# A three-block decoder layer on one core: the order in which the on-chip pools are laid in each partition

## The chip, the cores and the metric

The kernel runs on one core of one Trainium2 chip. The metric is the device time of one execution in microseconds (us). Three runs of the kernel before gave 2838.76, 2840.28 and 2841.42 us; the median is 2840.28 us.

## The reference

The reference takes 512 tokens of 1024 features, a memory of 256 rows, and runs three blocks one behind the other, all in float32.

- Block 1: a gated feed-forward layer (1024 to 2816 and back) with a layer norm; a pair of mixers side by side (a chunked gated delta rule of 8 heads with short convolutions, and a gated convolution of width 31), gated and joined; cross attention of 4 heads to the memory; a second gated feed-forward layer. Each part ends in a residual sum and a layer norm.
- Block 2: a retention branch and a sparse attention branch (compressed, selected and window keys) of 8 heads each, joined by one output matrix.
- Block 3: a neighbourhood attention branch and a latent attention branch, gated and joined, with a layer norm, and a third gated feed-forward layer with a layer norm.

Nearly all of the arithmetic is products of 512 tokens with weight matrices that are read once:

```python
def swiglu_ffn(x, w_gate, w_up, w_down):
    return (jax.nn.silu(x @ w_gate) * (x @ w_up)) @ w_down

x = layer_norm(DN_ALPHA * x + 0.5 * swiglu_ffn(x, ...), ln1_g[i], ln1_b[i])
proj = h @ w_in        # 1024 x 8208
```

## The kernel before, in words

**Split operands.** Every float32 operand of a large product is held as two tiles of the type float32r, the leading bits (hi) and the rest (lo). `mm3` (lines 192 to 196) makes one product from three matmuls: line 194 takes the lo part of the first operand with the hi part of the second, line 195 hi with lo, line 196 hi with hi. In `PE.matmul(o, lhsT, rhs)` the operand `lhsT` is stationary (128 columns are loaded into the array ahead of the matmul, the rows marked PEld in the profile) and `rhs` is moving (its 512 or 256 columns stream through). The profile names a matmul `mm<-moving,stationary`, so `mm<-x,wh` has an activation tile `x` moving over the weights `wh`, and `mm<-wh,x` has the weights moving over a stationary `x`.

**Weights.** `wload` (lines 269 to 275) fetches 512 KB of weights from HBM by one DMA of the SP queue into a tile `wr` of 1024 floats in each partition; `split` (lines 265 to 267) copies it to `wh` on ScalarE and subtracts to `wl` on VectorE or GpSimd. There are 2 tiles `wr`, 4 `wh` and 4 `wl`, all in the pool `wpool`, for the whole program.

**Activations.** The input of every block is an `Act` of 8 blocks of 128 features by 512 tokens. Those that outlive a phase are made by `xslot` (line 165) in the pool `xpool`: four tiles `x` of 4 blocks each, two for the hi parts and two for the lo parts. All others (`h`, `m`, `ma`, `y`, `ml`, `ra`, `rb`) lie in the pools of a phase, which `room` opens and closes.

**Two shapes of projection.** `feature_proj`, `swiglu` and `by_halves` (lines 306 to 347 and 460 to 487) put out features on partitions: the weights are stationary and 512 tokens of the activation move (256 in `by_halves`, which does the first half of the tokens of some blocks ahead of the second half). `token_proj` (lines 349 to 380) puts out tokens on partitions: 128 tokens of the activation are stationary and 512 columns of weights move. The order of all instructions on each engine's queue is the order in which the Python code emits them; it is written out by hand, in some phases by `interleave` (line 208), which takes turns between two generators by the TensorE time that each has been charged.

**Phases.** Feed-forward 1 is at 0 to about 350 us of the span; the delta rule with the gated convolution to about 800; the mixers' outputs and the cross attention to about 1300; feed-forward 2 to about 1650; block 2 to about 2060; block 3 to about 2480; feed-forward 3 to the end.

**Where tiles lie.** A pool takes a stretch of every partition's bytes, and the stretches follow each other in the order in which the pools are opened, each start rounded up to a multiple of 32 bytes. Four pools on chip are opened at the start (lines 118 to 124), and stay: `cpool` (constants), `xpool` (the four tiles `x`), `ypool` (small tiles and `t1`), `wpool`. The pools of the phases come behind them. In the built program the first pool starts at byte 16,512, and the stretches are:

| pool | first byte | bytes | tiles in it that large matmuls read |
|---|---|---|---|
| `cpool` | 16,512 | 4,640 | `ident` (transposes) |
| `xpool` | 21,152 | 32,768 | `x` |
| `ypool` | 53,920 | 7,208 | none |
| `wpool` | 61,152 | 40,960 | `wr` first, `wh` from 69,344, `wl` from 85,728 |
| pools of the phases | 102,112 | up to 126,464 | `h`, `m`, `ma`, `y`, `ml`, `ra`, `rb` and more |

The tiles `x`, `wr`, `wh`, `wl`, `h`, `m`, `ma` and `y` have 4,096 or 8,192 bytes in a partition, and the slices that a matmul takes of them start at multiples of 512 bytes from the tile's start. (For the 416-column projection of block 3 the step is 1,664 bytes.) So one number for each pool says where an operand starts within any 128 bytes: 32 for `x`, and 96 for the weights and for all tiles of the phases.

Of the kernel before, what the change touches and what calls it, by code (L numbers as in the profile page):

```python
# [14 lines left out]
PSUM = bass.MemoryType.PSUM  # L15
DRAM = bass.MemoryType.DRAM
# [10 lines left out]
BLOCK_STEP = 16 * 128 + 16  # L27
# [61 lines left out]
class Act:  # L89
    """Features on partitions, 512 tokens along: [128, 512] per block of 128 features, split exactly  # L90
    into the 12 leading bits (hi) and what is left (lo)."""
# [17 lines left out]
def kernel(ctx: ExitStack, tc: tile.TileContext, a: dict, out: bass.AP, upto=99):  # L109
# [7 lines left out]

    cpool = ctx.enter_context(tc.tile_pool(name="cpool", bufs=1))
    xpool = ctx.enter_context(tc.tile_pool(name="xpool", bufs=4))
    ypool = ctx.enter_context(tc.tile_pool(name="ypool", bufs=7))  # L120
    dpool = ctx.enter_context(tc.tile_pool(name="dpool", bufs=1, space=DRAM))

# [1 line left out]
    wpool = ctx.enter_context(tc.tile_pool(name="wpool", bufs=1))  # L124

# [1 line left out]
    now = {"lo": V, ("sb", "wr"): (wpool, 2), ("sb", "wh"): (wpool, 4), ("sb", "wl"): (wpool, 4)}  # L127

    class room:
        """SBUF tiles by tag."""  # L130
# [97 lines left out]
    def columns(rows):  # L228
        """Row vectors (dram [n, width <= 128]) turned into columns of one [128, 128] tile."""
        r = t1()  # L230
        V.memset(r, 0.0)
        at = 0
        for key, src in rows:
            n, w = src.shape
            S.dma_start(r[at:at + n, :w], src)
            cols[key] = at
            at += n
        p = tbank((128, T))
        PE.transpose(p[:, :128], r, ident)
        c = cpool.tile([128, 128], FT, name=nm("cols"))  # L240
        A.copy(c, p[:, :128])
        for key, src in rows:
            cols[key] = c[:, cols[key]:cols[key] + src.shape[0]]
# [36 lines left out]
    def to_act(x, act, tt, kk):  # L280
        """Half kk of token rows [128, 1024] into the columns of token tile tt."""
        p = tbank()
        for j in range(4):
            PE.transpose(p[:, j], x[:, (4 * kk + j) * 128:(4 * kk + j + 1) * 128], ident)
        h, l = (t[:, :, tt * 128:(tt + 1) * 128] for t in act.pair(kk))
        split(p, h, l)

    def inv_sqrt(o, x, scale, eps, n):
        """o = (x * scale + eps) ** -0.5"""
        V.tensor_scalar(o, x, scale, eps, OP.mult, OP.add)  # L290
        G.tensor_tensor(o, o, nhalf[:, :n], OP.pow)  # L291

    def layer_norm_rows(y, st, g, b, done):
        """Rows in place, given the statistics of both halves; done(i) after half i."""
        mv = tiny((128, 2), "mv")
        V.bn_aggr(mv, st)
        r = tiny((128, 1), "lr")
        inv_sqrt(r, mv[:, 1:2], 1.0, LN_EPS, 1)
        for i in range(2):
            yh, gh, bh = (t[:, i * 512:(i + 1) * 512] for t in (y, g, b))  # L300
            V.scalar_tensor_tensor(yh, yh, mv[:, 0:1], gh, OP.subtract, OP.mult)  # L301
            V.scalar_tensor_tensor(yh, yh, r, bh, OP.mult, OP.add)  # L302
            done(i)

# [1 line left out]
    def feature_proj(src, c0, nf, act, nk, consume, tag="pj", group=2):  # L306
        """consume(f, psum[128 features, 512]) for nf blocks of 128 columns from c0."""
        f = 0
        while f < nf:
            n = min(group, nf - f)  # L310
            ps = [bank(tag=tag) for _ in range(n)]
            step = 8 // n if nk > 8 // n else nk
            for k0 in range(0, nk, step):
                kn = min(step, nk - k0)
                h, l = wload(src, k0, kn, c0 + f * 128, n * 128)
                for i in range(n):
                    for k in range(kn):
                        cs = slice(i * 128, (i + 1) * 128)
                        mm3(ps[i], (h[:, k, cs], l[:, k, cs]), (act.hi(k0 + k), act.lo(k0 + k)),
                            k0 + k == 0, k0 + k == nk - 1)  # L320
                yield
            for i in range(n):
                consume(f + i, ps[i])
            f += n
            yield
# [3 lines left out]
    def by_halves(jobs, act):  # L329
        """For each (src, c0, banks): one block of 128 columns per bank, all over the first 256 tokens  # L330
        before the others."""
        ws = []
        for src, c0, banks in jobs:
            n = len(banks)
            ws.append(early.pop(0) if early else
                      [wload(src, k0, 8 // n, c0, n * 128, G) for k0 in range(0, 8, 8 // n)])
        for hf in range(2):
            ts_ = slice(hf * 256, (hf + 1) * 256)
            for (src, c0, banks), w in zip(jobs, ws):
                n = len(banks)  # L340
                for i in range(n):
                    cs = slice(i * 128, (i + 1) * 128)
                    for k in range(8):
                        h, l = w[k // (8 // n)]
                        mm3(banks[i][:, ts_], (h[:, k % (8 // n), cs], l[:, k % (8 // n), cs]),
                            (act.hi(k)[:, ts_], act.lo(k)[:, ts_]), k == 0, k == 7)
                yield

    def token_proj(src, c0, cn, act, nk, consume, tail=0, start=0, fine=False):
        """consume(tt, psum[128 tokens, cn]) for cn <= 512 columns from c0; the last `tail` chunks of  # L350
        rows go token tile by token tile."""
        per = max(1, min(nk, 1024 // cn))
# [41 lines left out]
    def block_out(act, nk, src, ys, alpha, norm, key, dest=None, tail=3, start=0):  # L394
        """x = norm(alpha * y + act @ src): rows to DRAM, columns split into a new Act."""
# [52 lines left out]
    def rms_rows(y):  # L448
        """Rows over their rms."""
# [10 lines left out]
    def swiglu(act, wg, gc, wu, uc, scale, h, f0, f1, first=None):  # L460
        """Blocks f0 .. f1 of silu(x wg) * (x wu) * scale."""
# [48 lines left out]
    # ================= first block =================  # L510
# [43 lines left out]
    # -- gated convolution branch --  # L554
# [64 lines left out]
    # -- gated delta rule --  # L619
# [67 lines left out]
    def gdn_rows(h):  # L687
        """q, k, v of one head: projection, short convolution, norms; k and q by features, k decayed and v
        by tokens."""
# [56 lines left out]
    def chunks(t, i):  # L746
        """In a scratch in which blocks of 16 along the diagonals are BLOCK_STEP apart: the chunks of head i."""
        src = t[0:1, 0:1]
        return bass.AP(tensor=src.tensor, offset=src.offset + i * 32 * BLOCK_STEP,
                       ap=[[128, 128], [8 * BLOCK_STEP, 4], [1, 128]])  # L750
# [27 lines left out]
    def gdn_blocks(h):  # L778
        """The inverse within blocks of 16 for heads h and h + 1, one block per partition."""
# [29 lines left out]
    def gdn_head(h):  # L809
# [6 lines left out]
        # blocks of the inverse joined two by two  # L816
# [113 lines left out]
    def gated(key, w, act, nk, bias, tag="pj"):  # L930
        """gate * (act w + bias), in place of the gate."""
# [22 lines left out]
    # -- cross attention --  # L954
# [53 lines left out]
    def soft(ps, P_, gate=None):  # L1008
        """Rows of scores (already scaled) to weights that sum to one (or to the gate)."""
# [62 lines left out]
    # ================= second block =================  # L1072
# [4 lines left out]
    def head_rms(p, nh):  # L1077
        """[128, heads, 64] of psum over its last axis -> 1 / rms, [128, 8]"""
# [15 lines left out]
    def nsa_keys():  # L1094
        """Keys of both branches and groups twice over the partitions, split."""
# [24 lines left out]
    def nsa_queries():  # L1120
        """Queries / 8: hi over lo for even heads, lo over hi for odd ones."""
# [115 lines left out]
    def nsa_attention():  # L1237
        """Heads 2j and 2j+1 share key group j // 2; the parts of one token tile follow those of the next
        one's scores."""
# [33 lines left out]
        def near(j, tt):  # L1273
            """Both branches, at most 256 keys."""
# [91 lines left out]
        units = []  # L1366
# [7 lines left out]
    def staggered(units):  # L1374
        """One more unit starts with every round, in which all that are under way take a step."""
# [12 lines left out]
    def overlapped(units, depth):  # L1388
        """Steps of `depth` consecutive units in turn."""
# [110 lines left out]
    # ================= third block =================  # L1500
    n3 = {}

    def na_q():
        """Queries / 8: hi over lo for even heads, lo over hi for odd ones; tiles of 16 columns by 8 rows."""
# [14 lines left out]
    def na_k():  # L1519
        """Keys: hi twice, lo once."""  # L1520
# [12 lines left out]
    def na_v():  # L1533
        """Values by keys, 8 rows by 32 columns for every tile of queries."""
# [21 lines left out]
    def rpb_tables():  # L1556
        """Relative biases between zeros, in DRAM, one copy of 8 key rows by 64 for every query of a tile; the
        copies lie so that the queries' windows start one stride apart."""
# [14 lines left out]
    def pair_attention(j, tt, scores, v, act, soft_one):  # L1573
        """Heads 2j and 2j+1 for the queries of token tile tt, over all keys."""
# [121 lines left out]
    def rope32(o, x, tt, nh):  # L1696
        """Rotates [128, nh, 32]: the first 16 by the row, the others by the column."""
# [73 lines left out]
    # ================= the program =================  # L1771
# [186 lines left out]
```

## Time and profile before

| what | value |
|---|---|
| median of three runs | 2840.28 us (2838.76 to 2841.42) |
| the profiled execution's own time | 2838.76 us |
| its span, first to last instruction | 2838.8 us |
| TensorE matmuls busy (13,600) | 2704.8 us, 95% of the span |
| TensorE weight loads busy | 2168.1 us, 76% |
| VectorE, ScalarE, GpSimd busy | 1430.9, 1047.9, 471.9 us |
| DMA engines busy, mean | 36.3% for the queue that brings the weights |
| granted TensorE clock, mean | 0.981 |

The span and the profiled execution's own time are the same to within a tenth of a microsecond, so nothing lies around the span. A busy time of matmuls counts overlapping records once. The duration of a single matmul record reaches into the next matmul, since they are pipelined, so the pace of a stretch is read from the distance between starts, not from a record's duration.

### The profile page before, as it was taken

Reading aid. Unit: us, or ns where it says so; the run is one execution under the profiler, and the core shown is the slowest. Engines: PE = TensorE matmul, PEld = TensorE weight load, DVE = VectorE, ACT = ScalarE, POOL = GpSimd, SP = SyncE. Lnnn points to the kernel's source line nnn. Section 1 sums busy time; section 2 is a strip of 40 time slices with the busy share of each in tenths; the row PEclk is TensorE's granted clock in tenths of the full one; section 3 lists DMA queues with packets and bytes.
Section 4 is the critical chain, followed back from the end, with each engine's and each line's share of the span. In section 5 each row is a group of like instructions: output and inputs, shape, how many; then the busy total and the mean of one; then the engine's idle time right before and its main releaser. Section 6 shows DMA issues by size and latency. Waiting matters only on the chain.

```text
span 2838.8 us, 34691 instructions
## 1 busy us (share of the span) xinstructions
PE 2704.8 (95%) x13600; PEld 2168.1 (76%) x13600; DVE 1430.9 (50%) x2516; ACT 1047.9 (37%) x1814; POOL 471.9 (17%) x325
## 2 busy tenths in 40 slices
PE   9999998889788999999999989999999999999998
PEld 7888876667576788888888867775777767888887
DVE  3232368977783456454232365575455464622324
ACT  4222234444443422433222254463256564322221
POOL 0101034343331011001101030131002001211010
PEclk9999999999899999999999999999999999999999
DMA  6333364457444343434333234312235223433322
GB/s 190 93 98 91 97 122 71 73 79 66 89 67 74 77 146 121 141 112 156 96 98 90 96 104 114 95 56 79 84 100 95 55 55 95 161 106 97 96 90 82
DMA packets 326036, 277.29 MB, mean 98 GB/s; under 512 B 50328, under 2 KB 278001, under 8 KB 325873
## 3 DMA queue, kind: packets, MB, share of 16 engines
q1 hardware_dynamic: 317808, 260.40, 36.3%
q10 hardware_dynamic: 8064, 14.68, 1.4%
q8 instruction: 107, 1.75, 0.3%
q14 instruction: 57, 0.46, 0.1%
HBM read 256.64 MB, written 20.49 MB: 98 GB/s over the span
## 4 chain that ended last, share of the span: by engine, by line
PE 47%; DVE 4%; POOL 1%; ACT 1%; DMA 1%; issue 1%; SPq 0%; DVEq 0%; ACTq 0%; POOLq 0%
PE mm L194 13%; PE mm L196 13%; PE mm L195 13%; PE mm L190 5%; DMA wr<-in_w_in 1%; DVE m L302 1%; PE mm L1590 0%; DVE wl L267 0%; ACT wh L266 0%; DVE m L301 0%; POOL t L950 0%; POOL hr L291 0%; PE mm L1348 0%; DVE st L429 0%; DVE m L413 0%
## 5 line engine op out<-in xcount | busy, mean ns | idle before, releaser
L267 DVE TENSOR_TENSOR wl<-wr,wh 128x1024 fp32r<-128x1024 f32 (+1 forms) x351 | 427.3, 1218 | 809.0 <-ACT wh L266 808.2
L194 PE MATMUL mm<-x,wl 128*128 128x512 f32 (+3 forms) x2072 | 809.1, 391 | 23.3 <-DVE xr L711 14.0
L195 PE MATMUL mm<-x,wh 128*128 128x512 f32 (+3 forms) x2072 | 805.0, 389 | 0.0
L196 PE MATMUL mm<-x,wh 128*128 128x512 f32 (+3 forms) x2072 | 804.7, 388 | 0.0
L266 ACT CAST wh<-wr 128x1024 fp32r<-128x1024 f32 (+2 forms) x425 | 436.2, 1027 | 802.6 <-PE mm L196 529.8
L194 PEld LDWEIGHTS mm<-x,wl 128*128 128x128 f32 (+2 forms) x2072 | 394.6, 190 | 109.9 <-DVE xr L711 14.9
L196 PEld LDWEIGHTS mm<-x,wh 128*128 128x128 f32 (+2 forms) x2072 | 394.5, 190 | 85.4 <-issue 2.7
L195 PEld LDWEIGHTS mm<-x,wh 128*128 128x128 f32 (+2 forms) x2072 | 394.9, 191 | 82.2 <-issue 1.9
L267 POOL TENSOR_TENSOR wl<-wr,wh 128x1024 fp32r<-128x1024 f32 x74 | 181.6, 2457 | 440.9 <-ACT wh L266 436.0
L267 POOL TENSOR_TENSOR h<-t,h 128x512 fp32r<-128x512 f32 x66 | 101.6, 1539 | 854.9 <-ACT h L266 854.9
L580 DVE SCALAR_TENSOR_TENSOR ma<-pad,cols,ma 128x512 f32<-128x512 f32 x240 | 227.7, 950 | 9.5 <-ACT ma L578 6.8
L196 PE MATMUL mm<-wh,h 128*128 128x512 f32 x528 | 205.6, 389 | 0.0
L195 PE MATMUL mm<-wl,h 128*128 128x512 f32 x528 | 205.6, 389 | 0.0
L194 PE MATMUL mm<-wh,h 128*128 128x512 f32 x528 | 205.6, 389 | 0.0
L196 PEld LDWEIGHTS mm<-wh,h 128*128 128x128 f32 x528 | 99.1, 188 | 20.6
L194 PEld LDWEIGHTS mm<-wh,h 128*128 128x128 f32 x528 | 99.1, 188 | 20.6
L195 PEld LDWEIGHTS mm<-wl,h 128*128 128x128 f32 x528 | 99.1, 188 | 20.6
L486 ACT ACTIVATE t<-mm 128x512 f32<-128x512 f32 x66 | 39.4, 597 | 132.3 <-PE mm L196 132.3
L487 DVE SCALAR_TENSOR_TENSOR t<-t,mm 128x512 f32<-128x512 f32 x66 | 45.4, 687 | 83.7 <-POOL h L267 57.0
L194 PE MATMUL mm<-m,wl 128*128 128x512 f32 (+1 forms) x224 | 81.8, 365 | 0.1
L196 PE MATMUL mm<-m,wh 128*128 128x512 f32 (+1 forms) x224 | 81.1, 362 | 0.0
L195 PE MATMUL mm<-m,wh 128*128 128x512 f32 (+1 forms) x224 | 81.0, 361 | 0.0
(441 smaller groups left out, 3658.1 us busy)
## 6 DMA issues: line engine op xcount, KB each, us to landing
wr<-in_w_in SPq DMA_DIRECT2D x122, 512.0 KB
wr<-in_ffn_wg SPq DMA_DIRECT2D x44, 512.0 KB
wr<-in_ffn_wu SPq DMA_DIRECT2D x44, 512.0 KB
wr<-in_ffn_wd SPq DMA_DIRECT2D x44, 512.0 KB
wr<-in_w_ffn_in SPq DMA_DIRECT2D x44, 512.0 KB
xd<-m ACTq DMA_DIRECT2D x48, 256.0 KB
m<-xd SPq DMA_DIRECT2D x24, 512.0 KB
wr<-in_w_ffn_out SPq DMA_DIRECT2D x22, 512.0 KB
```

The lines of the kernel that those rows point to most:

```text
L190: PE.matmul(o, lhsT, rhs, start=start, stop=stop)
L194: PE.matmul(o, lh[1], rh[0], start=start, stop=False)
L195: PE.matmul(o, lh[0], rh[1], start=False, stop=False)
L196: PE.matmul(o, lh[0], rh[0], start=False, stop=stop)
L266: A.copy(hi, src)
L267: (eng or V).tensor_sub(lo, src, hi.bitcast(FT))
L302: V.scalar_tensor_tensor(yh, yh, r, bh, OP.mult, OP.add)
L486: A.activation(sg, ps[0][f], AF.Silu)
L487: V.scalar_tensor_tensor(sg, sg, scale, ps[1][f], OP.mult, OP.mult)
L580: V.scalar_tensor_tensor(o, pad[:, j:j + T], tap31(j, c), o, OP.mult, OP.add)
```

## The change

The pools are opened in another order: `wpool` first, then `cpool`, then `ypool`, then `xpool`. `dpool` is in DRAM and takes no place on chip. The diff also deletes the text of comments and docstrings and keeps their lines, so that line numbers stay as they are; that leaves the program as it is.

```diff
+    wpool = ctx.enter_context(tc.tile_pool(name="wpool", bufs=1))
+
     cpool = ctx.enter_context(tc.tile_pool(name="cpool", bufs=1))
+    ypool = ctx.enter_context(tc.tile_pool(name="ypool", bufs=7))
     xpool = ctx.enter_context(tc.tile_pool(name="xpool", bufs=4))
-    ypool = ctx.enter_context(tc.tile_pool(name="ypool", bufs=7))
     dpool = ctx.enter_context(tc.tile_pool(name="dpool", bufs=1, space=DRAM))
 
-    # ---- weights as they come and split, for all phases ----
-    wpool = ctx.enter_context(tc.tile_pool(name="wpool", bufs=1))
-
-    # ---- scratch on chip, laid out anew for every phase ----
     now = {"lo": V, ("sb", "wr"): (wpool, 2), ("sb", "wh"): (wpool, 4), ("sb", "wl"): (wpool, 4)}
```

By the sizes in the table above the stretches become: `wpool` from 16,512, `cpool` from 57,472, `ypool` from 62,112, `xpool` from 69,344, and the pools of the phases from 102,112, where they are now. Within 128 bytes the weights then start at 0, `x` at 96, and the tiles of the phases at 96 as before.

## Rows read from the trace of the kernel before

**Rows 1.** The profile page's line of busy times by engine.

```profile
PE 2704.8 (95%) x13600; PEld 2168.1 (76%) x13600; DVE 1430.9 (50%) x2516; ACT 1047.9 (37%) x1814; POOL 471.9 (17%) x325
```

**Rows 2.** Busy time by stretch: the three feed-forward phases, the delta rule, and the rest. Columns: stretch, its length, then busy time (and number of instructions) of PE, PEld, DVE, ACT and POOL, granted clock, DMA share, GB/s.

```profile
0.00:350.00 350.00, 343.13 (x1566) 281.09 (x1567) 105.13 (x111) 101.78 (x126) 33.71 (x26) 1.00 0.38 114
350.00:800.00 450.00, 386.20 (x2134) 311.00 (x2133) 359.42 (x628) 185.24 (x313) 167.44 (x89) 0.94 0.53 82
800.00:1100.00 300.00, 281.38 (x1382) 229.25 (x1381) 163.70 (x246) 106.81 (x166) 51.51 (x35) 0.96 0.41 94
1300.00:1650.00 350.00, 350.00 (x1548) 285.40 (x1547) 106.60 (x110) 91.51 (x108) 37.42 (x24) 1.00 0.34 104
2480.00:2838.00 358.00, 350.13 (x1520) 284.10 (x1518) 116.90 (x131) 86.38 (x102) 38.00 (x26) 1.00 0.31 96
```

**Rows 3.** A stretch of feed-forward 1 in which `x` moves over weights, 512 columns each: its first and last two matmuls in the timeline of PE (start, duration, both in us).

```profile
30.26 0.39 PE L194 MATMUL mm<-x,wl 128*128 128x512 f32 x1
30.49 0.39 PE L195 MATMUL mm<-x,wh 128*128 128x512 f32 x1
...
147.39 0.39 PE L195 MATMUL mm<-x,wh 128*128 128x512 f32 x1
147.62 0.39 PE L196 MATMUL mm<-x,wh 128*128 128x512 f32 x1
```

**Rows 4.** The groups of PE instructions in the stretch from 30.26 to 147.8 us, by shape, with their number. The three groups of 512 columns are the matmuls of rows 3.

```profile
L194 PE MATMUL mm<-x,wl 128*128 128x512 f32 x168 | 66.2, 394 | 0.0
L195 PE MATMUL mm<-x,wh 128*128 128x512 f32 x168 | 66.2, 394 | 0.0
L196 PE MATMUL mm<-x,wh 128*128 128x512 f32 x168 | 66.2, 394 | 0.0
```

**Rows 5.** The stretch behind it, in which weights move over a stationary `h`, in the same view of PE in order of time.

```profile
147.86 0.39 PE L194 MATMUL mm<-wh,h 128*128 128x512 f32 x1
...
212.93 0.39 PE L196 MATMUL mm<-wh,h 128*128 128x512 f32 x1
```

**Rows 6.** A stretch in which an activation `m` of a phase's pool moves over weights, 512 columns each, in the same view.

```profile
989.42 0.40 PE L196 MATMUL mm<-m,wh 128*128 128x512 f32 x1
...
1058.14 0.39 PE L196 MATMUL mm<-m,wh 128*128 128x512 f32 x1
```

**Rows 7.** A stretch in which weights move over a stationary `x`, in the same view.

```profile
1779.98 0.40 PE L196 MATMUL mm<-wh,x 128*128 128x512 f32 x1
...
1793.04 0.39 PE L196 MATMUL mm<-wh,x 128*128 128x512 f32 x1
```

**Rows 8.** Two stretches with 256 moving columns over weights, `x` in the first and `m` in the second, in the same view.

```profile
394.44 0.28 PE L195 MATMUL mm<-x,wh 128*128 128x256 f32 x1
...
405.44 0.28 PE L196 MATMUL mm<-x,wh 128*128 128x256 f32 x1
...
1158.82 0.28 PE L194 MATMUL mm<-m,wl 128*128 128x256 f32 x1
...
1181.73 0.28 PE L196 MATMUL mm<-m,wh 128*128 128x256 f32 x1
```

**Rows 9.** Busy time in the stretches of rows 5 to 8, to count their matmuls; columns as in rows 2. A matmul that overlaps an edge is counted, so that the numbers of rows 6, 7 and the two of rows 8 hold one matmul ahead of the first row shown.

```profile
147.90:212.90 65.00, 65.00 (x288) 53.83 (x287) 19.83 (x20) 13.17 (x13) 1.93 (x2) 1.00 0.32 95
989.50:1058.20 68.70, 68.70 (x305) 56.85 (x304) 37.92 (x36) 20.92 (x25) 9.05 (x7) 1.00 0.44 140
1158.90:1181.80 22.90, 22.90 (x193) 22.90 (x192) 11.28 (x11) 10.37 (x12) 0.00 (x0) 1.00 0.51 147
394.50:405.50 11.00, 11.00 (x99) 11.00 (x99) 6.15 (x13) 4.36 (x6) 2.65 (x2) 1.00 0.67 209
1780.00:1793.10 13.10, 13.10 (x59) 10.69 (x57) 0.00 (x0) 2.76 (x4) 0.00 (x0) 1.00 0.14 40
```

**Rows 10.** The groups of line 194 in the whole span, by shape, with their numbers; lines 195 and 196 have as many of each. Columns: number, busy time and mean duration of one, idle time ahead and what ended it.

```profile
L194 PE MATMUL mm<-x,wl 128*128 128x512 f32 x1816 | 731.9, 403 | 22.6 <-DVE xr L711 14.0 <-DVE pad L575 6.6 <-ACT rg L1444 2.0
L194 PE MATMUL mm<-wh,h 128*128 128x512 f32 x528 | 205.6, 389 | 0.0
L194 PE MATMUL mm<-x,wl 128*128 128x256 f32 x240 | 70.9, 295 | 0.7 <-DVE wl L267 0.7
L194 PE MATMUL mm<-wh,x 128*128 128x512 f32 x160 | 65.1, 408 | 0.5 <-DVE x L1092 0.2 <-ACT wh L266 0.2
L194 PE MATMUL mm<-m,wl 128*128 128x512 f32 x160 | 63.7, 398 | 0.1
L194 PE MATMUL mm<-wh,m 128*128 128x512 f32 x104 | 41.1, 395 | 0.2 <-ACT t L1013 0.2
L194 PE MATMUL mm<-wh,y 128*128 128x512 f32 x64 | 25.1, 393 | 1.2 <-DVE m L940 1.2
L194 PE MATMUL mm<-wh,ma 128*128 128x512 f32 x64 | 25.0, 391 | 0.0
L194 PE MATMUL mm<-ml,wl 128*128 128x512 f32 x32 | 12.5, 390 | 0.0
```

**Rows 11.** The instructions that write or read a tile `x`, busy in the stretch of the delta rule; columns: PE, PEld, DVE, ACT, granted clock, DMA share, GB/s.

```profile
350.00:800.00 450.00, 290.78 (x1149) 209.25 (x1149) 5.30 (x8) 4.69 (x8) 0.94 0.53 82
```

## The prediction

> **What bounds the kernel now.** I began with the busy times: TensorE's matmuls are in flight for 95% of the span, and no other engine is over 50%, weight loads aside [rows 1]. Then I cut the span into phases. In feed-forward 2 TensorE is busy for 350 of 350 us, in the other two feed-forwards for all but 7 and 8 us, always at granted clock 1.00, the 2.4 GHz level; in the delta rule it is busy for 386 of 450 us, and VectorE for 359 [rows 2]. So outside the delta rule the time is a count of matmuls times the distance from one start to the next, and the question is what that distance hangs on.
>
> It is not the same everywhere. In 117 us of feed-forward 1 there are 3 x 168 matmuls that move 512 columns of `x` over weights, so 503 distances between 30.26 and 147.62 us [rows 3, 4]: 117.36 / 503 = 233.3 ns each. Right behind it weights move over `h`: (212.93 - 147.86) / 287 = 226.7 ns [rows 5, 9]. Shape, type, clock and the rate of fetched weights are alike. The orientation is not the reason: where `m` moves over the same weights, as `x` does, the distance is (1058.14 - 989.42) / 303 = 226.8 ns [rows 6, 9]. With `x` stationary it is (1793.04 - 1779.98) / 57 = 229.1 ns [rows 7, 9]. With 256 columns it turns round: `x` moves at (405.44 - 394.44) / 97 = 113.4 ns, `m` at (1181.73 - 1158.82) / 191 = 119.9 ns [rows 8, 9]. Apart from the stationary `x`, all these are whole multiples of 6.67 ns: 35, 34, 34, 17 and 18. 16 columns of four bytes, 64 bytes, take 6.67 ns at 2.4 GHz. So I read them as so many 64-byte pieces per matmul: 32 pieces for 512 columns, and two or three more. All operands now start 32 bytes past a multiple of 64, so that 512 columns touch 33 pieces; the last one or two come from how the read of the moving operand falls against the load of the next weights. What sets `x` apart from `m`, `h` and the weights is its place: it starts 32 bytes into a stretch of 128 bytes, all the others 96.
>
> **The change, part by part.** Instructions, their order, the DMAs, queues and waits: nothing is added, removed or moved. The four pools are opened before any tile is asked for, stay to the end, and fill the same bytes together; the pools of the phases begin at 102,112 as now, so the reuse of their tiles and its waits stay. SP's, ACT's and POOL's queues issue what they issue now. This is priced at nothing, and nothing has to cover it.
>
> What moves is where four kinds of tiles start. Constants and small tiles go in no long run of matmuls: nothing. The weights come to start at a multiple of 64 bytes (and of 128), and `x` comes to start at 96 of 128, as `m` and `h` do. That touches these matmuls [rows 10], three of each group counted there:
>
> 1. *`x` moving, 512 columns: 3 x 1816 = 5448.* Now 233.3 ns. No row shows the new pair, a moving operand at 96 over weights at 0. The near end is 226.7, if the place of `x` itself decides, for then it is `m`'s row; the other end is 233.3, if the two operands must lie alike within 128 bytes, for `x` and the weights differ now and differ after. I take 226.7: the moving operand, with 33 pieces, is the one whose pace is counted, and its new start is exactly that of `m` [rows 6]. 5448 x 6.6 = 36.0 us less.
> 2. *Weights moving over `h`, `m`, `y`, `ma`: 3 x (528 + 104 + 64 + 64) = 2280.* Now 226.7. An aligned start needs 32 pieces and not 33; if this counts in full it is 220.0, if the surplus is the load's it stays. No row has an aligned moving operand of this kind. I take the middle, 3.3 ns: 2280 x 3.3 = 7.5 us less (0 to 15).
> 3. *Weights moving over `x`: 3 x 160 = 480.* Now 229.1; `x` becomes like `h`, so 220.0 at best as in 2, and 229.1 at worst. I take 3.3 ns: 1.6 us less (0 to 4.4).
> 4. *`x` moving, 256 columns: 3 x 240 = 720.* By the argument of 1 it becomes `m`'s row: 6.6 ns more, 4.8 us more (0 to 4.8).
> 5. *`m` and `ml` moving over weights: 3 x (160 + 32) = 576.* The moving operand stays; I take nothing, between 6.6 ns less and 6.6 more: 3.8 us either way.
>
> Cover: in the delta rule 1149 instructions of PE have an `x` [rows 11], so 7.6 us of term 1 at most lie there. TensorE is idle for 64 us of that phase [rows 2] and some matmuls with `x` fill the time in which it would wait for VectorE. I count half as lost, 3.8 us. In the feed-forwards nothing hides behind TensorE: VectorE has 105 to 117 us of work in 350, ScalarE 86 to 102, DMA 31 to 38% [rows 2], so a matmul 3% quicker meets no new bound; what is late next is still the matmul.
>
> Sum: -36.0 - 7.5 - 1.6 + 4.8 + 3.8 = -36.5 us. The profiled execution's own time is 2838.8 us, 1.5 us under the median of the runs shown; 2838.8 - 36.5 = 2802.3, and I say **2802 us**.
>
> **The ports by the Trainium skill.** The rows show two paces for one shape and one clock, 233.3 and 226.8 ns, over the same weights [rows 3, 6]. The Trainium skill, "TensorE: Matmul & The Clock Gate", section "Step-by-step: what each phase is for", says that TensorE has two independent read ports into SBUF, so that loading the next weights takes no bandwidth from the running matmul. By that rule where the tiles lie is worth nothing, and the time would be 2838.8 us. The trace does not agree in so far as the place of `x` goes with 6.6 ns.
>
> **The rivals.** *Only the weights gain.* The pair decides, `x` and weights stay opposed within 128 bytes. `x` stays at 233.3 and 113.4; weights moving get their full piece, 2280 x 6.7 = 15.3 and 480 x 6.7 = 3.2; `m` over weights becomes opposed, 576 x 6.5 = 3.7 more. 2838.8 - 14.8 = 2824. For it: the 256-column rows show that no operand is slow by itself. *Both reads get shorter.* The weights' load, too, has a piece less when it starts aligned (8 and not 9). Then `x` falls to 33 pieces, 220.0: 5448 x 13.3 = 72.5, with 15.3 and 4.4 beside it, and about 8 lost in the delta rule: some 84 less, 2755. Against it: every row has at least one surplus piece. *Low bytes are slow.* `x` lies lowest of all large operands now; then the weights inherit that. `x` moving becomes the pace of today's stationary one, 229.1: 5448 x 4.2 = 22.9 less; weights moving become 233.3: 2280 x 6.6 + 480 x 4.2 = 17.0 more; term 5 pays 576 x 2.3 = 1.3. 2834. Against it: with 256 columns `x` is the quick one. *No effect,* as by independent ports, or because the profile's starts differ for another reason: 2839. Against it is the steadiness, 503 distances without one out of line. *Slower.* The opposition spreads and alignment gives no piece back. The place is TensorE's moving read beside its weight load: weights moving over `h` pay what they pay over `x`, 2280 x 2.4 = 5.5; `m` pays what `x` pays, 3.7; `x` keeps 233.3 and may pay more. 2848 or above. It decides if the distance of `x` over weights stays above 231.6 (9.2 us / 5448 = 1.7 ns under today's). For it: no row has a pair at 0 and 96, and 64 bytes apart was the worse one in two of three shapes.
>
> **How the numbers follow.** Forecast, between 2784 and 2822: 0.47. Only the weights: 0.22. Both shorter: 0.08. Low bytes: 0.06, and 0.04 for no effect; slower 0.13. Leaving out "both shorter" and "slower" leaves about 0.79, from the forecast's lower bound, widened by terms 2 and 5 and half of the way to the deep case, to no effect: 2768 to 2842. A measurement of this kernel can tell about 0.2%, 5.7 us, from no change. Faster is the forecast, only the weights and both shorter: 0.77; within 0.2% are low bytes and no effect: 0.10; slower 0.13. The first three have the sign in common; within the likeliest alone the range is 2784 to 2822.
>
> **What would show it.** Right: the same counts of instructions in all groups; in feed-forward 1 the stretch of 504 matmuls with `x` takes 114 us and not 117.4, at 226.7 ns; the stretch of 288 with `h` at 220 to 226.7 ns; 256 columns of `x` at 120. The phases with TensorE at 100% shorten by 2 to 3%, the delta rule by less. Wrong: `x` at 233.3, which is "only the weights" if `h` falls to 220, and "slower" if `h` goes to 229; `x` at 229 and `h` at 233, which is low bytes. Wrong in another way would be a change of engine durations or of waits for DMA, since this prices neither.

## The result, and the profile after

The change makes the kernel slower by about half a per cent: 2855.39 us, the median of four runs (2853.92 to 2856.71), against 2840.85 us for the kernel before (2838.76 to 2843.42). The ratio is 1.0055, 95% interval 1.0043 to 1.0068. The forecast was 2802 us, with a range from 2768 to 2842, so the sign and the range were wrong. The profiled execution took 2854.75 us, its span is 2852.9 us, and the mean granted clock was 0.983 (0.981 before).

The instructions stand in the same order on every engine, and their counts are the same. The page's line of busy times, to hold against [rows 1]:

```profile
PE 2726.2 (96%) x13600; PEld 2174.7 (76%) x13600; DVE 1434.7 (50%) x2516; ACT 1047.6 (37%) x1814; POOL 473.5 (17%) x325
```

TensorE's matmuls are busy for 21.4 us more; its weight loads moved by 6.6 us, and no other engine by more than 4. TensorE's idle time fell from 2838.8 - 2704.8 = 134.0 to 2852.9 - 2726.2 = 126.7 us, so 7.3 us of the extra time lies where it used to wait, and 14.1 us lengthen the span. By stretch, with the columns of [rows 2]:

```profile
0.00:350.00 350.00, 344.23 (x1547) 281.16 (x1548) 103.60 (x108) 100.83 (x125) 33.82 (x26) 1.00 0.35 113
350.00:800.00 450.00, 386.59 (x2101) 310.77 (x2100) 358.34 (x613) 183.15 (x304) 168.74 (x89) 0.93 0.52 82
```

In 350 us of feed-forward 1, TensorE is as busy as before and gets through 1547 matmuls, not 1566. Some 6 of these 19 are due to a start that is 1.5 us later; the others are missing because the matmuls themselves are further apart. The timeline of PE has the first and last matmul of the stretches of [rows 3], [rows 5], [rows 8] and [rows 6], and of [rows 7]:

```profile
31.74 0.40 PE L194 MATMUL mm<-x,wl 128*128 128x512 f32 x1
...
149.11 0.39 PE L196 MATMUL mm<-x,wh 128*128 128x512 f32 x1
149.34 0.39 PE L194 MATMUL mm<-wh,h 128*128 128x512 f32 x1
...
216.57 0.40 PE L196 MATMUL mm<-wh,h 128*128 128x512 f32 x1
...
399.52 0.28 PE L195 MATMUL mm<-x,wh 128*128 128x256 f32 x1
...
411.15 0.28 PE L196 MATMUL mm<-x,wh 128*128 128x256 f32 x1
...
995.22 0.40 PE L196 MATMUL mm<-m,wh 128*128 128x512 f32 x1
...
1065.91 0.39 PE L196 MATMUL mm<-m,wh 128*128 128x512 f32 x1
...
1167.98 0.28 PE L194 MATMUL mm<-m,wl 128*128 128x256 f32 x1
...
1190.90 0.28 PE L196 MATMUL mm<-m,wh 128*128 128x256 f32 x1
...
1793.22 0.40 PE L196 MATMUL mm<-wh,x 128*128 128x512 f32 x1
...
1806.58 0.39 PE L196 MATMUL mm<-wh,x 128*128 128x512 f32 x1
```

Divided by the same numbers of distances as before, these give:

| matmuls | before, ns | after, ns |
|---|---|---|
| `x` over weights, 512 columns | 233.3 | 117.37 / 503 = 233.3 |
| weights over `h`, 512 | 226.7 | 67.23 / 287 = 234.2 |
| `m` over weights, 512 | 226.8 | 70.69 / 303 = 233.3 |
| weights over `x`, 512 | 229.1 | 13.36 / 57 = 234.4 |
| `x` over weights, 256 | 113.4 | 11.63 / 97 = 119.9 |
| `m` over weights, 256 | 119.9 | 22.92 / 191 = 120.0 |

What was to become quick stayed slow, and what was quick became slow.

### The profile page after: what moved, and what is told of

Same layout as the page of the kernel before. It is cut to its first block, busy times and chain, and to the rows that moved or that the text cites. A ratio compares the mean times of both kernels' runs of the same rounds, so it can differ in the third digit from the quotient of the medians.

```text
span 2852.9 us, 34691 instructions
## 1 busy us (share of the span) xinstructions
PE 2726.2 (96%) x13600; PEld 2174.7 (76%) x13600; DVE 1434.7 (50%) x2516; ACT 1047.6 (37%) x1814; POOL 473.5 (17%) x325
## 4 chain that ended last, share of the span: by engine, by line
PE 48%; DVE 4%; POOL 1%; ACT 1%; issue 1%; DMA 0%; DVEq 0%; SPq 0%; POOLq 0%; ACTq 0%
PE mm L194 13%; PE mm L196 13%; PE mm L195 13%; PE mm L190 5%; DVE m L302 1%; PE mm L1590 0%; DVE m L301 0%; POOL t L950 0%; PE mm L1348 0%; DVE st L429 0%; DVE m L413 0%; DMA wr<-in_w_in 0%; POOL hr L291 0%; DVE wl L267 0%; PE mm L284 0%
## 5 line engine op out<-in xcount | busy, mean ns | idle before, releaser
L196 PE MATMUL mm<-wh,h 128*128 128x512 f32 x528 | 209.5, 397 | 0.0
L194 PE MATMUL mm<-wh,h 128*128 128x512 f32 x528 | 209.4, 397 | 0.0
```

Of the source, the lines that this page charges most:

```text
L194: PE.matmul(o, lh[1], rh[0], start=start, stop=False)
L196: PE.matmul(o, lh[0], rh[0], start=False, stop=stop)
```

## The experiments

Each of the ten kernels differs from the kernel before only in the order of the pools on chip and in unused tiles (`gap1`, `gap2`) that shift what follows; e9 also lengthens a tile. The edits are shown against the kernel before. To follow them, two numbers are needed: where an operand starts, and how far the start of the moving operand is from that of the stationary one. The table has both within 256 bytes, worked out as in the table of pools; `ph` stands for all tiles of the phases. Two operands are called alike when their distance is 0.

| kernel | `x` | weights | `ph` | `x` over weights | weights over `ph` | `ph` over weights | ratio to before (95%) |
|---|---|---|---|---|---|---|---|
| before | 160 | 224 | 224 | 192 | 0 | 0 | 1 |
| after | 224 | 128 | 224 | 96 | 160 | 96 | 1.0055 (1.0043 to 1.0068) |
| e1 | 224 | 224 | 224 | 0 | 0 | 0 | 0.9914 (0.9899 to 0.9929) |
| e2 | 0 | 0 | 0 | 0 | 0 | 0 | 0.9920 (0.9905 to 0.9935) |
| e3 | 96 | 224 | 96 | 128 | 128 | 128 | 1.0049 (1.0033 to 1.0066) |
| e4 | 64 | 128 | 128 | 192 | 0 | 0 | 0.9998 (0.9988 to 1.0008) |
| e5 | 224 | 224 | 224 | 0 | 0 | 0 | 0.9907 (0.9888 to 0.9927) |
| e6 | 224 | 224 | 160 | 0 | 64 | 192 | 0.9937 (0.9915 to 0.9958) |
| e7 | 224 | 192 | 96 | 32 | 96 | 160 | 1.0065 (1.0045 to 1.0086) |
| e8 | 224 | 0 | 64 | 224 | 192 | 64 | 1.0047 (1.0032 to 1.0063) |
| e9 | 224 | 224, `wl` 0 to 192 on | 224 | mixed | mixed | mixed | 0.9997 (0.9985 to 1.0010) |
| e10 | 160 | 128 | 224 | 32 | 160 | 96 | 1.0057 (1.0040 to 1.0074) |

**e1: half of the change.** `xpool` and `ypool` change places and the weights stay where they were, so that `x`, weights and phases start alike.

```diff
-    xpool = ctx.enter_context(tc.tile_pool(name="xpool", bufs=4))
     ypool = ctx.enter_context(tc.tile_pool(name="ypool", bufs=7))
+    xpool = ctx.enter_context(tc.tile_pool(name="xpool", bufs=4))
```

> Only the order of two pools is undone against the kernel before: constants, small tiles, x, weights. The weights and all tiles of the phases stay where they were before; x moves up by 7,232 bytes and now starts at 96 within 128 bytes, as all other operands do. Theory A, the pair must start alike within 128 bytes: x moving over weights goes from 233.3 to 226.7 ns, with 256 columns from 113.4 to 120 ns, weights over x from 229.1 to 226.7: -36.0 + 4.8 - 1.2 us, a few of them lost in the delta rule, so about 2812 us. Theory B, operands in the low bytes (under some 60,000) are slow: x still lies at 28,384 to 61,152, so 233.3 and 113.4 ns stay and the time is 2841 us.

Measured: 2814.46 us, where the kernel before took 2839.47. The page's line of busy times:

```profile
PE 2678.9 (95%) x13600; PEld 2173.7 (77%) x13600; DVE 1436.6 (51%) x2516; ACT 1047.9 (37%) x1814; POOL 473.3 (17%) x325
```

and the stretches with `x` moving 512 and 256 columns in the timeline of PE:

```profile
30.59 0.40 PE L193 MATMUL mm<-x,wl 128*128 128x512 f32 x1
...
144.63 0.39 PE L195 MATMUL mm<-x,wh 128*128 128x512 f32 x1
...
388.25 0.28 PE L194 MATMUL mm<-x,wh 128*128 128x256 f32 x1
...
399.88 0.28 PE L195 MATMUL mm<-x,wh 128*128 128x256 f32 x1
```

114.04 / 503 = 226.7 ns: `x` takes the pace that `m` and `h` had. With 256 columns it is 119.9, where it was 113.4 before. So half of what the change does is a gain of 0.9%, and what turns it into a loss is the move of the weights. `x` still lies below the weights, as in the kernel before, which speaks against "low bytes are slow".

**e2: alike, at another start.** As e1, with 32 unused bytes ahead of `xpool`, so that all large operands start at a multiple of 256.

```diff
-    xpool = ctx.enter_context(tc.tile_pool(name="xpool", bufs=4))
     ypool = ctx.enter_context(tc.tile_pool(name="ypool", bufs=7))
+    gap1 = ctx.enter_context(tc.tile_pool(name="gap1", bufs=1)).tile([128, 8], FT, name="gap1")
+    xpool = ctx.enter_context(tc.tile_pool(name="xpool", bufs=4))
```

> As the run with everything at 96, with 32 bytes left free ahead of x, so that x, the weights and all tiles of the phases start at a multiple of 128 bytes. Theory A with nothing else: all pairs alike, so the same distances as there, 226.7 and 120 ns, and about 2812 us. Theory A with the count of 64-byte pieces: an aligned start saves a piece of each moving operand, 220.0 ns with 512 columns and 113.4 with 256, on some 9000 matmuls, 60 us less: about 2755 us. Theory B: x is still low, 2841 us.

Measured: 2816.99 us, which can't be told from e1. The timeline of PE, `x` over weights and weights over `h`:

```profile
30.75 0.40 PE L194 MATMUL mm<-x,wl 128*128 128x512 f32 x1
...
144.79 0.39 PE L196 MATMUL mm<-x,wh 128*128 128x512 f32 x1
145.02 0.39 PE L194 MATMUL mm<-wh,h 128*128 128x512 f32 x1
...
210.07 0.39 PE L196 MATMUL mm<-wh,h 128*128 128x512 f32 x1
```

Both are at 226.7 ns (114.04 / 503 and 65.05 / 287). An aligned operand gives back no 64-byte piece: where operands start is worth nothing by itself, as far as these two kernels go.

**e3: alike within 128 bytes only.** Weights first, `x` and the phases 128 bytes off them within 256.

```diff
+    gap1 = ctx.enter_context(tc.tile_pool(name="gap1", bufs=1)).tile([128, 24], FT, name="gap1")
+    wpool = ctx.enter_context(tc.tile_pool(name="wpool", bufs=1))
     cpool = ctx.enter_context(tc.tile_pool(name="cpool", bufs=1))
-    xpool = ctx.enter_context(tc.tile_pool(name="xpool", bufs=4))
     ypool = ctx.enter_context(tc.tile_pool(name="ypool", bufs=7))
+    gap2 = ctx.enter_context(tc.tile_pool(name="gap2", bufs=1)).tile([128, 8], FT, name="gap2")
+    xpool = ctx.enter_context(tc.tile_pool(name="xpool", bufs=4))
...
-    wpool = ctx.enter_context(tc.tile_pool(name="wpool", bufs=1))
```

> The changed order (weights first) with 96 bytes left free ahead of the weights and 32 ahead of x, so that weights, x and the tiles of the phases all start at 96 within 128 bytes; the weights stay low in the partition. Within 512 bytes the weights start at 224 and the others at 352, so they are not alike there. Theory A: 226.7 ns for x, m and h with the weights, about 2812 us. Theory B, low bytes: weights low, so all pairs stay as in the changed kernel, 233.3 and 234.3 ns, 2855 us. If alike within 512 bytes is what counts: not 226.7.

Measured: 2854.62 us, as slow as the change. The timeline of PE, `x` over weights and weights over `h`:

```profile
31.61 0.39 PE L195 MATMUL mm<-x,wl 128*128 128x512 f32 x1
...
148.49 0.40 PE L197 MATMUL mm<-x,wh 128*128 128x512 f32 x1
148.72 0.40 PE L195 MATMUL mm<-wh,h 128*128 128x512 f32 x1
...
215.69 0.39 PE L197 MATMUL mm<-wh,h 128*128 128x512 f32 x1
```

116.88 / 503 = 232.4 ns, and weights over `h` are at 66.97 / 287 = 233.3. The prediction counted starts within 128 bytes, and by that count these operands are alike. Either the period is longer than that, or weights that lie low are slow. e3 alone leaves this open.

**e4: the relations of before, at other starts.**

```diff
-    xpool = ctx.enter_context(tc.tile_pool(name="xpool", bufs=4))
     ypool = ctx.enter_context(tc.tile_pool(name="ypool", bufs=7))
+    gap1 = ctx.enter_context(tc.tile_pool(name="gap1", bufs=1)).tile([128, 24], FT, name="gap1")
+    xpool = ctx.enter_context(tc.tile_pool(name="xpool", bufs=4))
+    gap2 = ctx.enter_context(tc.tile_pool(name="gap2", bufs=1)).tile([128, 16], FT, name="gap2")
```

> The order constants, small tiles, x, weights, with free bytes so that the weights and the tiles of the phases start at 0 within 128 bytes and x at 64: every operand starts at a multiple of 64 bytes, and x is opposed to the weights by 64. Theory A: weights over h and m over weights alike, 226.7 ns (220.0 if an aligned start saves a piece); x over weights unlike, 233.3 ns (226.7 if it saves one), with 256 columns 113.4. Time 2841 us, or with the piece about 2785. Theory B: as in the kernel before, 2841 us.

Measured: 2840.02 us against 2839.47, no change. The timeline of PE:

```profile
31.72 0.39 PE L195 MATMUL mm<-x,wl 128*128 128x512 f32 x1
...
149.08 0.40 PE L197 MATMUL mm<-x,wh 128*128 128x512 f32 x1
149.31 0.40 PE L195 MATMUL mm<-wh,h 128*128 128x512 f32 x1
...
214.38 0.39 PE L197 MATMUL mm<-wh,h 128*128 128x512 f32 x1
```

233.3 and 226.7 ns, the paces of before, with every large operand 96 bytes further back within 256. The paces went with the distance between the two operands and not with where they start. The changed kernel and e1 say the same of `x` from the other side: in both it starts at 224, and over the weights it takes 233.3 ns in the one and 226.7 in the other. So the place of `x`, the prediction's reason for its largest term, does not set its pace.

**e5: weights first, as in the change, but all alike.**

```diff
+    gap1 = ctx.enter_context(tc.tile_pool(name="gap1", bufs=1)).tile([128, 24], FT, name="gap1")
+    wpool = ctx.enter_context(tc.tile_pool(name="wpool", bufs=1))
     cpool = ctx.enter_context(tc.tile_pool(name="cpool", bufs=1))
-    xpool = ctx.enter_context(tc.tile_pool(name="xpool", bufs=4))
     ypool = ctx.enter_context(tc.tile_pool(name="ypool", bufs=7))
+    gap2 = ctx.enter_context(tc.tile_pool(name="gap2", bufs=1)).tile([128, 104], FT, name="gap2")
+    xpool = ctx.enter_context(tc.tile_pool(name="xpool", bufs=4))
...
-    wpool = ctx.enter_context(tc.tile_pool(name="wpool", bufs=1))
```

> The changed order, weights first and low in the partition, with 96 bytes left free ahead of the weights and 416 ahead of x, so that the weights, x and the tiles of the phases all start at 224 within 512 bytes. Theory C, only the difference between the starts of the moving and the stationary operand counts, taken within 512 bytes: zero everywhere, so 226.7 ns with 512 columns, 120 ns with 256, and about 2814 us as with everything at 96 in the unchanged place. Theory D, weights that lie low in the partition are slow, wherever they start: distances of 232 to 234 ns stay, about 2855 us.

Measured: 2813.41 us against 2838.54. The timeline of PE, `x` over weights:

```profile
32.34 0.40 PE L195 MATMUL mm<-x,wl 128*128 128x512 f32 x1
...
146.38 0.39 PE L197 MATMUL mm<-x,wh 128*128 128x512 f32 x1
```

226.7 ns again. The weights lie as low as in the change, and the order of the pools is the change's own. This settles what e3 left open: it is not the place low in the partition. e1, e2 and e5, the three kernels with all operands alike, can't be told from each other, and all three beat both the kernel before and the change (e6 does too, by less).

**e6, e7, e8: the size of the step.** All three have `cpool`, `ypool`, `xpool`, then an unused tile, `wpool` and another unused tile. The gaps are 256 and 192 bytes in e6 (shown), 480 and 160 in e7, 288 and 64 in e8.

```diff
-    xpool = ctx.enter_context(tc.tile_pool(name="xpool", bufs=4))
     ypool = ctx.enter_context(tc.tile_pool(name="ypool", bufs=7))
+    xpool = ctx.enter_context(tc.tile_pool(name="xpool", bufs=4))
+    gap1 = ctx.enter_context(tc.tile_pool(name="gap1", bufs=1)).tile([128, 64], FT, name="gap1")
+    wpool = ctx.enter_context(tc.tile_pool(name="wpool", bufs=1))
+    gap2 = ctx.enter_context(tc.tile_pool(name="gap2", bufs=1)).tile([128, 48], FT, name="gap2")
...
-    wpool = ctx.enter_context(tc.tile_pool(name="wpool", bufs=1))
```

> Order constants, small tiles, x, 256 free bytes, weights, 192 free bytes, phases. Moving minus stationary within 512 bytes: x over weights 256, m over weights 192, weights over h 320 (minus 192). Theory C with a period of 512: x not alike, about 232 to 234 ns, so 2840 us or more. Theory C with a period of 256: x alike, 226.7 ns, and weights over h as a difference of 64, 229.1 ns, m over weights as minus 64, 233.3 ns: about 2823 us. Theory D: weights high, so 226.7 ns for all that start where they like, 2814 us.

Measured: 2821.16 us. The timeline of PE, `x` over weights, weights over `h`, and `m` over weights:

```profile
31.96 0.40 PE L195 MATMUL mm<-x,wl 128*128 128x512 f32 x1
...
146.00 0.39 PE L197 MATMUL mm<-x,wh 128*128 128x512 f32 x1
146.23 0.39 PE L195 MATMUL mm<-wh,h 128*128 128x512 f32 x1
...
211.92 0.39 PE L197 MATMUL mm<-wh,h 128*128 128x512 f32 x1
...
983.77 0.40 PE L197 MATMUL mm<-m,wh 128*128 128x512 f32 x1
...
1054.47 0.39 PE L197 MATMUL mm<-m,wh 128*128 128x512 f32 x1
```

`x`, now 256 bytes off the weights within 512, is at 226.7 ns, as if alike. Weights over `h`, 64 off within 256 and 320 within 512, are at 65.69 / 287 = 228.9, where weights over `x` were at 229.1 before with 64 within both. So with 512 columns the period is 256. `m`, 192 off, is at 70.70 / 303 = 233.3 ns, which is the pace that `x` had at 192 before. So the same distance makes the same price for another tile.

> Order constants, small tiles, x, 480 free bytes, weights, 160 free bytes, phases. Moving minus stationary within 512 bytes: x over weights 32, m over weights 160, weights over h minus 160. Theory C does not say what half a 64-byte piece does: between 226.7 (a piece is what counts) and 234.3 ns (any difference counts) for x; weights over h as in the changed kernel, 232 to 234 ns. So 2830 to 2868 us. Theory D: 226.7 ns, 2814 us.

Measured: 2856.68 us. The timeline of PE, `x` at 32 and `m` at 160:

```profile
31.27 0.40 PE L195 MATMUL mm<-x,wl 128*128 128x512 f32 x1
...
148.63 0.39 PE L197 MATMUL mm<-x,wh 128*128 128x512 f32 x1
...
991.47 0.39 PE L197 MATMUL mm<-m,wh 128*128 128x512 f32 x1
...
1062.45 0.40 PE L197 MATMUL mm<-m,wh 128*128 128x512 f32 x1
```

233.3 and 234.3 ns. 32 bytes off already cost the whole price.

> Order constants, small tiles, x, 288 free bytes, weights, 64 free bytes, phases. Moving minus stationary within 512 bytes: x over weights 224, m over weights 64, weights over h minus 64. Theory C: weights over h take 233.3 ns, as x over weights did at minus 64 in the kernel before; m over weights 229.1 ns, as weights over x did at 64; x somewhere from 226.7 to 234.3 ns. So 2830 to 2870 us. Theory D: 2814 us.

Measured: 2852.08 us. The timeline of PE, `x` at 224 and `m` at 64:

```profile
30.86 0.39 PE L195 MATMUL mm<-x,wl 128*128 128x512 f32 x1
...
148.22 0.40 PE L197 MATMUL mm<-x,wh 128*128 128x512 f32 x1
...
990.69 0.39 PE L197 MATMUL mm<-m,wh 128*128 128x512 f32 x1
...
1060.04 0.39 PE L197 MATMUL mm<-m,wh 128*128 128x512 f32 x1
```

233.3 and 228.9 ns. One tile does not fit. `ml`, which block 3 moves over weights and which e8 puts at 64 too, takes (2414.1 - 2392.4) / 93 = 233.3 ns, counted from its first matmul on line 195 to its last there:

```profile
L195 PE MATMUL mm<-ml,wl x32: 397/397/398, 2392.4 to 2414.1; 128*128 128x512 f32 x32
```

Put together from e1 to e8, e10 and the two kernels, with the distance taken as the start of the moving operand less that of the stationary one, within 256 bytes:

| distance, bytes | 512 columns, ns | 256 columns, ns |
|---|---|---|
| 0 | 226.7 | 120.0 |
| 32 | 233.3 | 116.7 |
| 64 | 228.9 to 229.1, `ml` 233.3 | 117.8 |
| 96 | 233.3 | 120.0 |
| 128 | 232.4 to 233.3 | 118.6 |
| 160 | 234.2 to 234.4 | 118.7 |
| 192 | 233.3 | 113.4 for `x`, 117.8 for `m` in e6 |
| 224 | 233.3 | 118.3 |

For 512 columns one number says nearly all: alike is best, 64 bytes is near it but for `ml`, everything else costs 6 to 8 ns. For 256 columns it does not: at 192 there are two paces. Within 512 bytes the two differ, `x` being at 448 there and `m` in e6 at 192; no run tells whether that, or something else about the tiles, makes the difference.

**e9: which of the two weights counts.** As e1, with the tiles `wl` 64 bytes longer than needed, so that the four of them start at 0, 64, 128 and 192 bytes from the rest. One matmul in three with `x` moving (line 193 here, 194 before) then has, in three cases of four, unlike weights of its own, and another has them loaded behind it.

```diff
-        raw, hi, lo = work("wr", (128, 1024)), work("wh", (128, 1024), FR), work("wl", (128, 1024), FR)
+        raw, hi, lo = work("wr", (128, 1024)), work("wh", (128, 1024), FR), work("wl", (128, 1040), FR)
```

> The kernel with everything at 96 (constants, small tiles, x, weights), but each tile wl has 64 bytes more, so that the four wl tiles start 0, 64, 128 and 192 bytes on within 256 bytes, while wr, wh, x and the phases are alike. Line 194 then has an unlike stationary operand in three of four cases, lines 195 and 196 none. Theory P, a matmul's distance hangs on its moving operand and its own weights: the distance from line 194 to line 195 goes from 226.7 to 229 to 233 ns, the two others stay. Theory N, it hangs on its moving operand and the weights that are loaded meanwhile, those of the matmul behind it: the distance from line 196 to the next line 194 grows, and that from line 194 to 195 stays. By both the time is about 10 us over that kernel, 2824 us (1816 x 3.7 ns for x over wl, 984 x 3.7 ns for wl over the others).

Measured: 2839.16 us, 15 us above the 2824 that was expected. The page's line of busy times has PE at 2702.6 us, 23.7 more than e1:

```profile
PE 2702.6 (95%) x13600; PEld 2175.6 (77%) x13600; DVE 1437.0 (51%) x2516; ACT 1048.0 (37%) x1814; POOL 474.3 (17%) x325
```

The timeline of PE, `x` over weights:

```profile
31.74 0.40 PE L193 MATMUL mm<-x,wl 128*128 128x512 f32 x1
...
147.48 0.40 PE L195 MATMUL mm<-x,wh 128*128 128x512 f32 x1
```

115.74 / 503 = 230.1 ns. Sorted by the distance of `x` over its `wl` (64 where `wl` lies 192 further on), over the whole span and without the distances above 260 ns, the mean from start to start is:

| `x` over `wl`, bytes | from its own matmul to the next, ns | from the matmul ahead of it to its own, ns |
|---|---|---|
| 0 | 227.5 | 227.9 |
| 64 | 233.4 | 230.7 |
| 128 | 233.8 | 232.4 |
| 192 | 235.2 | 229.3 |

The third distance of each triple, with alike weights on both sides, is 228.3. So unlike weights lengthen two distances, the one in which they are in use and the one in which they come to be used, and neither a theory of a matmul's own weights nor one of the next weights is enough. For the same reason the table above holds only where all the weights lie alike: a distance of 64 for `wl` alone costs 5.9 ns and 2.8 here, where 64 for all weights cost 2.2 to 2.4 a matmul. The expectation priced one distance of the three, and the expected loss was too small for that. (230.1 - 226.7) x 5448 = 18.5 us is the price for `x`; `wl` moving over `h` pays beside it.

**e10: the other half of the change.** Weights first, `xpool` and `ypool` in their old order.

```diff
+    wpool = ctx.enter_context(tc.tile_pool(name="wpool", bufs=1))
     cpool = ctx.enter_context(tc.tile_pool(name="cpool", bufs=1))
...
-    wpool = ctx.enter_context(tc.tile_pool(name="wpool", bufs=1))
```

> Half of the change: the weights go first, x and the small tiles keep their order (weights, constants, x, small tiles), no free bytes. Moving minus stationary within 256 bytes: x over weights 32, m over weights 96, weights over h minus 96, weights over x minus 32. By the distances of the runs so far, theory C with a period of 256: x 233.3 and, with 256 columns, 116.7 ns, m 233.3, weights over h 234.3, weights over x 233.3 ns; that is the changed kernel but for 720 x 3.3 = 2.4 us, about 2853 us. Theory D, low weights are slow, is out by the run with weights first and alike; if x is what costs when it follows the weights, this kernel is quicker than 2841 us.

Measured: 2854.20 us, where the table of distances gave 2853. The timeline of PE:

```profile
31.41 0.39 PE L193 MATMUL mm<-x,wl 128*128 128x512 f32 x1
...
148.76 0.40 PE L195 MATMUL mm<-x,wh 128*128 128x512 f32 x1
149.00 0.39 PE L193 MATMUL mm<-wh,h 128*128 128x512 f32 x1
...
216.23 0.39 PE L195 MATMUL mm<-wh,h 128*128 128x512 f32 x1
```

233.3 and 234.2 ns. The loss of the whole change is all in this half. The swap of `xpool` and `ypool`, worth 0.9% alone (e1), is worth nothing once the weights have been moved to 128, 96 bytes off the tiles of the phases.

## Why the prediction was wrong, point by point

**What bounds the kernel.** Right. The time is a count of matmuls by the distance between their starts, and the starts of the operands set this distance. VectorE and ScalarE are as busy as before (1434.7 and 1047.6 us).

**Term 1, `x` moving, 36.0 us less: the step that failed.** It chose between two ends, the place of `x` itself and the relation of `x` to the weights, and took the first. The second holds. Before, `x` was 192 off the weights, after it is 96 off, and both cost 233.3 ns, so that nothing came of the 36.0 us. The prediction named this end, and dropped it because the moving operand was "the one whose pace is counted"; that reason did not come from a row. The rows that could have spoken were there: weights over `x`, the same two tiles in the other roles, were at 229.1 where weights over `h` were at 226.7. A theory of the moving operand alone has no place for this difference. Nor do the paces come in whole pieces of 6.67 ns, as the prediction read them: 228.9 and 232.4 ns are 34.3 and 34.9 of them.

**Term 2, weights over `h` and its like, 7.5 us less.** Wrong in sign. No aligned piece exists (e2). The weights were alike with these tiles, and the change took that away: 2280 x (234.2 - 226.7) = 17.1 us more, outside the range of 0 to 15 less that was given. This is the larger part of the loss.

**Term 3, weights over `x`.** 480 x (234.4 - 229.1) = 2.5 us more, not 1.6 less, for the same reason.

**Term 4, 256 columns of `x`.** Right in number, 119.9 ns, 4.7 us more; but not by its reason, since in e7 `x` has the same start, 224, and is at 116.7 ns, 32 off the weights.

**Term 5, `m` and `ml`.** Its bad end came: 576 x 6.5 = 3.7 us more.

**Sum and cover.** 0 + 17.1 + 2.5 + 4.7 + 3.7 = 28.0 us at the full paces, and some 1.4 more for weights over `ra` and `rb` (192 matmuls at 7.5 ns), which the five terms leave out; the span grew by 14.1. The starts of the same matmuls before and after show where the rest went. Ahead of the first long stretch there are 1.5 us (30.26 to 31.74): 144 matmuls of term 4 stand there, 0.9 us, and the rest does not go with the pace, for this start lies at 30.59 in e1 and at 32.34 in e5. At 394.44 the lag is 5.1 us, at 989.42 it is 5.8. Between them lie the delta rule and most of the mixers' outputs, but only 98 matmuls of term 4 and 80 of term 5, 1.2 us at the full paces, so there was little to cover. At 1158.82 it is 9.2. At 1779.98, behind feed-forward 2, it is 13.2, and 4.0 of this is what 528 weights over `h` cost at 7.5 ns; the matmuls between these two starts cost 8.2 us at the full paces, by their counts, so half of that was covered. In feed-forward 3 the groups of weights over `h` have these ranges of starts, before:

```profile
L194 PE MATMUL mm<-wh,h x176: 388/389/397, 2598.3 to 2829.3; 128*128 128x512 f32 x176
```

and after:

```profile
L194 PE MATMUL mm<-wh,h x176: 391/397/400, 2608.8 to 2843.8; 128*128 128x512 f32 x176
```

The lag is 10.5 us at the first and 14.5 at the last: again 4.0 in the phase, while blocks 2 and 3 gave back 2.7 and hid some 6.6 us that their matmuls cost at the full paces. TensorE has idle time there, in block 2 of the kernel after 17.3 us (columns of [rows 2]):

```profile
1650.00:2060.00 410.00, 392.73 (x2109) 289.59 (x2108) 236.63 (x579) 182.24 (x439) 77.89 (x69) 1.00 0.29 88
```

So about half of the loss was covered, the share that the prediction took for its gain in the delta rule, but here it was found for the most part in the cross attention and in blocks 2 and 3. What TensorE waited for there is not shown.

**The rivals.** "Slower" came true, by its own sign: `x` over weights stayed above 231.6 ns, and `m` paid what it priced. Its 2848 was too low because it priced weights over `h` at 229.1, the one cheap distance that the rows before showed; the change made it 234.2. It was given 0.13. "Only the weights gain" had the relation right, and the period and the aligned piece wrong: e3 and e2 speak against these. "Low bytes" falls with e5, "both reads get shorter" with e2. "No effect" falls with all of them: e1 and e3 run the same instructions on the same data and differ by 40.2 us. The rule of the Trainium skill beside which it stood, "TensorE: Matmul & The Clock Gate", section "Step-by-step: what each phase is for", with its two independent read ports, does not account for this either: in e9 the distance behind a matmul whose own weights are alike grew from 227.9 to 232.4 ns when the next weights were 128 off. Whether it is the weight load that disturbs the running matmul, or something else that hangs on the pair, no run here shows.

**What stays open.** Why the distance within 256 bytes matters, and why 64 is nearly free for most tiles and not for `ml`, is not shown; nor what gives 256 columns two paces at 192. The numbers above say only what is paid.

## What to carry to other kernels

Where TensorE is the bound and its operands are float32r, read the distance between the starts of matmuls by pair of tiles, not by tile: two tiles that are each quick with one partner can be slow with another. Lay the pools so that all tiles that meet in large matmuls start alike within 256 bytes; here this took the swap of two lines and gave 0.9%, and the two other layouts that kept it, e2 and e5 with their unused tiles, did as well. When a trace leaves two readings of a difference, look for a row with the same two tiles in other roles before choosing.

## What the runs showed of the hardware that was not expected

- One shape at one clock (granted 1.00, the 2.4 GHz level) runs at 226.7 to 234.4 ns for 512 columns, and the distance of the two operands' starts within 256 bytes goes with the pace of all tiles but one; 32 bytes off cost 6.6 ns, 64 bytes 2.2 to 2.4 (6.6 for `ml`), and 256 bytes nothing.
- With 256 columns alike operands are not the quickest: 120.0 ns, where 192 off gave 113.4 for `x`.
- The start of an operand is worth nothing by itself: with all at 224 within 256 bytes the kernel took 2814.46 us (e1), with all at 0 it took 2816.99 (e2).
- The weights that come next and those in use both count (e9): shifting the tiles `wl` alone, by up to 192 bytes, took back the whole 0.9% that e1 had gained.
